# A trunk step in split fp32r on one core: the prompt's convolution as ScalarE products added in pairs by VectorE, with the weight split, w_in's tail and two norms rearranged

## The chip, the cores and the metric

The kernel runs on one core of a Trainium2 chip. The metric is device time in microseconds of one execution; the figure before is 2956.64, the median of three runs. PE is TensorE, DVE is VectorE, ACT is ScalarE, POOL is GpSimd and SP is the engine that issues the DMAs.

## The reference

One inference step of a hybrid decoder layer for 256 prompt positions and 8 x 8 sample positions, 320 columns in all, at model width 2048:

```
x1 = layer_norm(ALPHA * x + 0.5 * swiglu_ffn(x, ffn1), ln1)
proj = x1 @ w_in            # q, k, v, o, gates, glu_a, glu_b, gate_a, gate_b
h_a = mlstm_branch(q, k, v, o, ...)
u = glu_a * sigmoid(glu_b)  # depthwise convolution, 31 taps, over the positions
y = conv(concat([buf, u])) + conv_b;  h_b = silu(layer_norm(y, conv_ln))
mix = (sigmoid(gate_a) * h_a + sigmoid(gate_b) * h_b) @ w_out
x2 = layer_norm(ALPHA * x1 + mix, ln2)
y = layer_norm(ALPHA * x2 + 0.5 * swiglu_ffn(x2, ffn2), ln3)
```

The outputs are y, the new matrix memories and normalisers of the mLSTM branch, and the last 30 inputs of the convolution.

## The kernel before, in words

**Matrix products.** Activations stand as 16 tiles (k = 0 to 15) of 128 features by 320 positions. Weights come as blocks of 128 x 128, in the order in which they are used, in chunks of 8 blocks (one DMA of 512 KB each, `Stream.load`). Every fp32 product is made of three fp32r matmuls per block (`mm3`, L213 to L215): high part of the weights by the high and by the low part of the activations, then low part of the weights by the high part. `Stream._split` makes the parts: ACT copies the high part (whi, L148) and DVE subtracts it (wlo, L149), in halves of a chunk, 128 x 512, with five buffers for each and three halves made ahead.

**The order of the work.** There are 784 chunks: ffn1 (264), w_in (224), w_out (32), ffn2 (264). A group of output blocks has one accumulator in PSUM for each; the pool has five accumulators (acc) and three smaller tiles (sm). After every four blocks `tick` advances each lane by a step: lane 0 holds the gates, the heads and later the states, lane 1 norms and the finishing of the convolution, lanes 2 and 3 the convolutions by turns. `drain` emits steps of lanes until a condition holds. From the order in which the program is written, the scheduler of the tile framework makes each engine's queue; engines work in their queue's order and wait for one another by semaphores.

**w_in.** `w_in_schedule` writes the groups: first a and g of columns 0 and 1 (the inputs of the convolution), then for each further column a, g and some of q, k, v, o, ga of the heads; then a tail, gb for 16 columns, and last `oga(3)`, that is o and ga of head 3 in eight groups. A gb group's accumulator is emptied by ACT's tanh (`tanh_half`, L248), and its result multiplies the finished convolution, after its norm.

**The convolution** (`conv`, L602 to L627). ACT makes tap 0, then DVE 30 products with addition (L622, 128 x 256). The samples' part (`conv_sample`) is a product of 128 x 992 and a reduction, in two halves. Two convolutions run by turns. The 16 results are normed (`Norm`): DVE subtracts the mean (L1134) and multiplies (L1135), and ACT makes r = 1 / sqrt(v) by a logarithm and an exponential (`rsqrt`, L239 to L243).

**Starting on a norm that isn't finished** (`first_group`). The first group of w_in (4 accumulators) and of ffn2 (4) use "early" tiles eh and el, made from values to which the norm has not been applied, with two extra columns; mean and r are put in afterwards on the result (`normed`: w, late; L287 to L290). Meanwhile the normed tiles are made: L1134, L1135, xh on ACT (L500), xl on DVE (L501). In ffn2 `states` starts behind this group: 64 small matmuls (cps, L914), each followed by a DVE step into a memory tile c (L915) which DMAs load and store.

**The last norm** (`last_norm`). Centring of four tiles is done by PE (L473, L474: the tile by the identity, minus the mean of the sum), of four by POOL and of eight by DVE (L467); DVE and POOL multiply by r (L486); ACT applies gain and offset to eleven (L493) and DVE to five (L491); a DMA stores each.

Of the kernel before, what the change touches and what calls it, by code (L numbers as in the profile page):

```python
# [14 lines left out]
P = 128  # L15
# [5 lines left out]
NB = 8  # L21
# [94 lines left out]
class Stream:  # L116


    AHEAD = 3
    RAW_AHEAD = 3  # L120

    def __init__(self, nc, pool, src, n_blocks):
        self.nc, self.pool, self.src = nc, pool, src
        self.n_chunks, self.n_parts = n_blocks // CB, n_blocks // PB
        self.raw, self.parts = {}, {}
        self.next_raw = self.next_split = 0
        self.i = 0
# [12 lines left out]
    def _split(self, p):  # L140
        nc = self.nc
        c, j = divmod(p, CB // PB)
        raw = self.raw[c][:, j * PB * P:(j + 1) * PB * P]
        if (j + 1) * PB == CB:
            del self.raw[c]
        hi = self.pool.tile([P, PB * P], F32R, tag="whi", name="whi", bufs=5)
        lo = self.pool.tile([P, PB * P], F32R, tag="wlo", name="wlo", bufs=5)
        nc.scalar.activation(hi, raw, AF.Copy)  # L148
        nc.vector.tensor_tensor(out=lo, in0=raw, in1=hi.bitcast(F32), op=ALU.subtract)  # L149
        self.parts[p] = (hi, lo)  # L150

    def advance(self, p):
        while self.next_raw < min(p // (CB // PB) + self.RAW_AHEAD + 1, self.n_chunks):
            for _ in self.load():
                pass
        while self.next_split < min(p + self.AHEAD + 1, self.n_parts):
            self._split(self.next_split)
            self.next_split += 1

    def get(self):  # L160
        p, j = divmod(self.i, PB)
        if j == 0:
            self.parts.pop(p - 1, None)
            self.advance(p)
        self.i += 1
        hi, lo = self.parts[p]
        s = slice(j * P, (j + 1) * P)
        return hi[:, s], lo[:, s]


class Kernel:
    TICK = 4

    def __init__(self, tc, a):
        self.tc, self.nc, self.a = tc, tc.nc, a
        self.lanes = [collections.deque() for _ in range(4)]
# [40 lines left out]
    def gemm(self, accs, xs):  # L217

        n = len(xs)
        for k, (xh, xl) in enumerate(xs):  # L220
# [73 lines left out]
    def first_group(self, count, norm, name):  # L294

        accs = [self.acc(T + 2) for _ in range(count)]
        ys = []

        def tiles():
            for k in range(KD):  # L300
                ys.append(self.affine_split(*norm.scaled(k, name)))
                norm.z[k] = None
                yield

        self.later(tiles(), 1)
        self.gemm(accs, norm.early)
        self.drain((1,), lambda: len(ys) == KD)
        norm.early.clear()
        return [self.normed(ps, norm) for ps in accs], ys
# [9 lines left out]
    def build(self):  # L319
        tc, nc, a = self.tc, self.nc, self.a  # L320
        with (
# [11 lines left out]
            xs = []  # L333

            def x(n):
                k = len(xs)
                n = min(n, KD - k)
                raw = mp.tile([P, n * T], F32, tag="c0", name="xraw", bufs=3)
# [17 lines left out]
    def consts(self, cp):  # L356
# [3 lines left out]
        sel = self.mp.tile([ROWS, H * P], F32, tag="c0", name="selraw", bufs=3)  # L360
# [59 lines left out]
    def ffn(self, n, xs, norm=None):  # L420
# [5 lines left out]
        for kind, q, ms in ffn_schedule():  # L426
            if kind == "up":
                if xs is None:
                    accs, xs = self.first_group(2 * len(ms), norm, "ln2")
                    self.later(self.states())  # L430
# [28 lines left out]
    def last_norm(self, norm):  # L459

        nc = self.nc
        by_pe, by_pool = (0, 4, 8, 12), (3, 7, 11, 15)
        z, d = norm.z, {}

        def centre(k):
            eng = nc.gpsimd if k in by_pool else nc.vector
            eng.tensor_tensor(out=z[k], in0=z[k], in1=norm.mean, op=ALU.subtract)  # L467
            d[k] = z[k]

        with self.tc.issue_after(norm.sums.ins):  # L470
            for k in by_pe:
# [3 lines left out]
        for k in (3, 7, 1):  # L475
            centre(k)
        with self.tc.issue_after(norm.var.ins):
            for k in (2, 5, 6, 9, 11, 15):
                centre(k)
        first = None  # L480
        for k in list(d) + [k for k in range(KD) if k not in d]:
            with self.tc.issue_after((norm.last if k in d else first).ins):
                if k not in d:
                    centre(k)
                eng = nc.gpsimd if k in by_pool else nc.vector
                mul = eng.tensor_tensor(out=z[k], in0=d[k], in1=norm.r, op=ALU.mult)  # L486
                if eng is nc.vector and first is None:
                    first = mul
                g, b = self.scol("ln3_g", -0.5, k), self.col("ln3_b", k)
                if k % 3 == 1:  # L490
                    nc.vector.tensor_scalar(z[k], z[k], g, b, op0=ALU.mult, op1=ALU.add)  # L491
                else:
                    nc.scalar.activation(z[k], z[k], AF.Identity, scale=g, bias=b)  # L493
                nc.sync.dma_start(out=self.a["yT"][k], in_=z[k])
# [20 lines left out]
    def gates(self, g8):  # L515
# [60 lines left out]
        rows = mp.tile([H, R_N], F32, tag="c0", name="rows", bufs=3)  # L576
# [27 lines left out]
    def conv(self, i, acc_a, acc_g, done):  # L604
# [12 lines left out]
        nc.scalar.activation(y[:, :SEQ], pu[:, :SEQ], AF.Identity, scale=self.cw[:, i, 0:1], bias=bias)  # L617
        yield
        yield
        yp = y[:, :SEQ]  # L620
        for w in range(1, CW):
            nc.vector.scalar_tensor_tensor(out=yp, in0=pu[:, w:w + SEQ], scalar=self.cw[:, i, w:w + 1], in1=yp, op0=ALU.mult, op1=ALU.add)  # L622
            yield
            if w == 3:
                nc.sync.dma_start(out=a["conv_p"][i], in_=pu[:, SEQ:])
                nc.sync.dma_start(out=a["conv_s"][i], in_=us[:, :, NS:])
            if w in (8, 16):  # L627
                self.conv_sample(i, us, y, (w // 8 - 1) * NB // 2)
                yield
        nc.scalar.activation(y[:, SEQ:], y[:, SEQ:], AF.Identity, bias=bias)  # L630
        done(y)

    def conv_sample(self, i, us, y, b0):

        nc, n = self.nc, NB // 2
        x = self.mp.tile([P, n, NS, CW], F32, tag="taps", name="taps", bufs=1)
# [21 lines left out]
    def head(self, h, q, k, v):  # L658
# [6 lines left out]
        def load(b):  # L665
            if b < NB:
                c0[b] = mp.tile([P, 2, DV], F32, tag="c0", name="c0", bufs=3)
# [98 lines left out]
        cn = mp.tile([P, 2, DV], F32, tag="c0", name="cn", bufs=3)  # L766
# [113 lines left out]
    def states(self):  # L880
# [8 lines left out]
        def load(u):  # L889
            if u < H * NB:  # L890
                h, b = divmod(u, NB)
                c0[u] = mp.tile([P, 2, DV], F32, tag="c0", name="c0", bufs=3)
# [32 lines left out]
    def mixer(self, before):  # L925
# [33 lines left out]
        for n, group in enumerate(w_in_schedule()):  # L959
            if ys is None:  # L960
                accs, ys = self.first_group(len(group), before, "ln1")
# [3 lines left out]
            for (x, i), ps in zip(group, accs):  # L965
# [9 lines left out]
                elif x == "g":  # L975
                    self.later(self.conv(i, pend.pop(i), ps, functools.partial(conv_done, i)), 2 + i % 2)
                    self.step(self.lanes[2 + i % 2])
                elif x == "gb":
                    s = self.tanh_half(ps)
                    self.drain((2, 3, 1), lambda: self.silu_done > i)  # L980
# [239 lines left out]
```

## Time and profile before

| | us |
|---|---|
| median of 3 runs | 2956.64 (2956.19 to 2958.51) |
| the profiled execution | 2956.17 |
| its span in the trace | 2954.4 |
| PE / DVE / ACT / POOL busy | 2898.7 / 1894.8 / 1340.6 / 70.0 |
| granted PE clock, mean | 0.992 |

A row of a timeline gives start, length, engine, line, operation, output from inputs, shapes and count; a bracket behind it gives idle time before and what ended it. A row of groups gives busy time in us and the mean of one in ns. A row of waits gives the total in us, how often, and the longest. A row of stretches gives each engine's busy time with its count of instructions, then the granted clock of PE. Merged rows run back to back, so their length by their count is the pace of a queue; a single row is longer, since the end of one overlaps the start of the next.

### The profile page before, as it was taken

Reading aid. Unit: us, or ns where it says so; the run is one execution under the profiler, and the core shown is the slowest. Engines: PE = TensorE matmul, PEld = TensorE weight load, DVE = VectorE, ACT = ScalarE, POOL = GpSimd, SP = SyncE. Lnnn points to the kernel's source line nnn. Section 1 sums busy time; section 2 is a strip of 40 time slices with the busy share of each in tenths; the row PEclk is TensorE's granted clock in tenths of the full one; section 3 lists DMA queues with packets and bytes.
Section 4 is the critical chain, followed back from the end, with each engine's and each line's share of the span. In section 5 each row is a group of like instructions: output and inputs, shape, how many; then the busy total and the mean of one; then the engine's idle time right before and its main releaser. Section 6 shows DMA issues by size and latency. Waiting matters only on the chain.

```text
span 2954.4 us, 50389 instructions
## 1 busy us (share of the span) xinstructions
PE 2898.7 (98%) x19582; PEld 2868.9 (97%) x19582; DVE 1894.8 (64%) x3495; ACT 1340.6 (45%) x2384; POOL 70.0 (2%) x76
## 2 busy tenths in 40 slices
PE   9999999999999899999999989999999999999997
PEld 9999999999999899999999989998999999999997
DVE  5544444444448999989989885587454455455447
ACT  5433433433445555554554564454433433433444
POOL 0100000000000000000000000201100000000001
PEclk9999999999999999999999999999999999999999
DMA  6444444444444456554645634446455555555542
GB/s 220 150 150 150 150 150 150 150 150 151 150 150 139 125 154 194 153 170 144 202 136 174 194 116 150 150 140 223 150 183 185 198 185 196 201 181 196 176 150 103
DMA packets 171521, 483.22 MB, mean 164 GB/s; under 512 B 51308, under 2 KB 54252, under 8 KB 171280
## 3 DMA queue, kind: packets, MB, share of 16 engines
q1 hardware_dynamic: 171280, 480.00, 49.8%
q8 instruction: 153, 2.51, 0.4%
q14 instruction: 88, 0.72, 0.1%
HBM read 453.04 MB, written 26.89 MB: 162 GB/s over the span
## 4 chain that ended last, share of the span: by engine, by line
PE 96%; DVE 3%; ACT 1%; issue 0%; DMA 0%; DVEq 0%; SPq 0%; ACTq 0%
PE acc L213 31%; PE acc L214 31%; PE acc L215 31%; PE ip L822 1%; DVE z L1135 0%; PE cps L914 0%; DVE wlo L149 0%; PE num L843 0%; DVE cy L1135 0%; DVE z L486 0%; DVE xl L501 0%; PE tv L722 0%; PE sp L690 0%; PE num L214 0%; DVE cy L1134 0%
## 5 line engine op out<-in xcount | busy, mean ns | idle before, releaser
L149 DVE TENSOR_TENSOR wlo<-wraw,whi 128x512 fp32r<-128x512 f32 x1568 | 1084.6, 693 | 879.6 <-ACT whi L148 873.1
L148 ACT ACTIVATE whi<-wraw 128x512 fp32r<-128x512 f32 x1568 | 988.3, 631 | 1441.9 <-PE acc L214 1326.5
L213 PE MATMUL acc<-xh,whi 128*128 128x320 f32 x4480 | 1391.6, 311 | 25.7 <-ACT th L248 15.3
L214 PE MATMUL acc<-xl,whi 128*128 128x320 f32 x4480 | 1388.6, 310 | 6.9 <-DVE xl L501 6.9
L215 PE MATMUL acc<-xh,wlo 128*128 128x320 f32 x4480 | 1386.5, 310 | 2.7 <-DVE wlo L149 2.7
L213 PEld LDWEIGHTS acc<-xh,whi 128*128 128x128 f32 x4480 | 846.8, 189 | 31.0 <-ACT th L248 16.0
L214 PEld LDWEIGHTS acc<-xl,whi 128*128 128x128 f32 x4480 | 846.8, 189 | 13.8 <-DVE xl L501 8.6
L215 PEld LDWEIGHTS acc<-xh,wlo 128*128 128x128 f32 x4480 | 844.6, 189 | 7.1 <-DVE wlo L149 3.2
L213 PE MATMUL acc<-hh,whi 128*128 128x320 f32 x1408 | 434.4, 310 | 0.3 <-ACT whi L148 0.3
L214 PE MATMUL acc<-hl,whi 128*128 128x320 f32 x1408 | 434.0, 309 | 0.0
L215 PE MATMUL acc<-hh,wlo 128*128 128x320 f32 x1408 | 432.9, 309 | 0.0
L214 PEld LDWEIGHTS acc<-hl,whi 128*128 128x128 f32 x1408 | 264.7, 188 | 0.7
L213 PEld LDWEIGHTS acc<-hh,whi 128*128 128x128 f32 x1408 | 264.7, 188 | 0.6 <-ACT whi L148 0.6
L215 PEld LDWEIGHTS acc<-hh,wlo 128*128 128x128 f32 x1408 | 264.2, 188 | 0.0
L622 DVE SCALAR_TENSOR_TENSOR cy<-pu,cw,cy 128x256 f32<-128x256 f32 x480 | 220.9, 480 | 1.2
L448 DVE SCALAR_TENSOR_TENSOR z<-acc,z 128x320 f32<-128x320 f32 x128 | 62.7, 490 | 51.5 <-PE acc L215 49.8
L214 PE MATMUL acc<-ml,whi 128*128 128x320 f32 x256 | 79.2, 310 | 0.0
L213 PE MATMUL acc<-mh,whi 128*128 128x320 f32 x256 | 79.0, 309 | 0.0
L215 PE MATMUL acc<-mh,wlo 128*128 128x320 f32 x256 | 78.7, 309 | 0.0
L438 DVE TENSOR_TENSOR h<-s,acc 128x320 f32<-128x320 f32 x86 | 42.0, 488 | 51.9 <-ACT s L436 51.9
L315 POOL TENSOR_TENSOR z<-xh,xl 128x320 f32<-128x320 f32 x48 | 60.0, 1256 | 621.3 <-DVE h L438 357.1
L436 ACT ACTIVATE s<-acc 128x320 f32<-128x320 f32 x86 | 37.6, 438 | 69.0 <-PE acc L215 69.0
(290 smaller groups left out, 1655.1 us busy)
## 6 DMA issues: line engine op xcount, KB each, us to landing
wraw<-in_wst SPq DMA_DIRECT2D x783, 512.0 KB, 3.3
c<-in_C SPq DMA_DIRECT2D x64, 512.0 KB, 4.4
out_C_s<-c SPq DMA_DIRECT2D x32, 512.0 KB, 3.3
out_yT<-z SPq DMA_DIRECT2D x16, 160.0 KB, 1.9
out_C_p<-cn SPq DMA_DIRECT2D x4, 512.0 KB, 3.0
kv<-vst SPq DMA_DIRECT2D x8, 256.0 KB, 4.9
vst<-kv SPq DMA_DIRECT2D x8, 256.0 KB, 3.2
us<-in_cache SPq DMA_DIRECT2D x16, 120.0 KB, 3.1
```

Of the source, the lines that this page charges most:

```text
L148: nc.scalar.activation(hi, raw, AF.Copy)
L149: nc.vector.tensor_tensor(out=lo, in0=raw, in1=hi.bitcast(F32), op=ALU.subtract)
L213: mm(ps, hi, xh, start=first, stop=False)
L214: mm(ps, hi, xl, start=False, stop=False)
L215: mm(ps, lo, xh, start=False, stop=last)
L315: self.nc.gpsimd.tensor_tensor(out=t, in0=hi.bitcast(F32), in1=lo.bitcast(F32), op=ALU.add)
L436: nc.scalar.activation(s, accs[2 * j], AF.Silu)
L438: nc.vector.tensor_tensor(out=hh, in0=s, in1=accs[2 * j + 1], op=ALU.mult)
L448: nc.vector.scalar_tensor_tensor(out=z[m], in0=ps, scalar=0.5 / ALPHA, in1=z[m], op0=ALU.mult, op1=ALU.add)
L622: nc.vector.scalar_tensor_tensor(out=yp, in0=pu[:, w:w + SEQ], scalar=self.cw[:, i, w:w + 1], in1=yp, op0=ALU.mult, op1=ALU.add)
L822: mm(ip[:32, :], qc[j][:, bs], x, start=j == 0 and n == 0, stop=j == 1 and n == 1)
```

## The change

Four things change together.

1. `conv`: ACT makes 30 products in pairs, side by side in tiles of 128 x 2 x 256; DVE adds the pairs (14 adds of 128 x 512), makes the last tap and adds the two halves. The samples' part comes in four parts of 128 x 496. One lane holds all convolutions one after another, and before the third and every later one starts, the last but one is drained.
2. `Stream`: whole chunks are split at once (128 x 1024; the first two chunks still in halves), with three buffers for each part, two chunks ahead.
3. `w_in_schedule`: in each step the other groups come ahead of a and g, and the tail is `oga(3)`, then the 16 gb groups.
4. `first_groups`: in ffn2 the first two up groups (4 accumulators, then one accumulator and one small PSUM tile) use the early tiles, and `states` starts behind the second. `last_norm`: PE centres nine tiles, DVE seven, POOL none; DVE multiplies in the order of k, and ACT applies gain and offset to all 16.

The ring c0 of large tiles goes from three buffers to two, with some of its users on another tag.

```
-        groups += [[("a", i)], [("g", i)]]
         upto = len(others) * (n + 1) // len(steps)
         groups += [[x] for x in others[done:upto]]
         done = upto
-    tail = [("gb", j) for j in range(KD)] + oga(3)
+        groups += [[("a", i)], [("g", i)]]
+    tail = oga(3) + [("gb", j) for j in range(KD)]
...
+        hi = self.pool.tile([P, CB * P], F32R, tag="whi", name="whi", bufs=3)
+        lo = self.pool.tile([P, CB * P], F32R, tag="wlo", name="wlo", bufs=3)
+        n = PB * P if c < 2 else CB * P
+        for i in range(0, CB * P, n):
+            s = slice(i, i + n)
+            nc.scalar.activation(hi[:, s], raw[:, s], AF.Copy)
+            nc.vector.tensor_tensor(out=lo[:, s], in0=raw[:, s], in1=hi[:, s].bitcast(F32), op=ALU.subtract)
...
+        accs = [self.acc(T + 2) for _ in range(4)]
         self.later(tiles(), 1)
-        self.gemm(accs, norm.early)
+        self.gemm(accs, norm.early, not more)
+        if more:
+            yield [self.normed(ps, norm) for ps in accs]
+            del accs
+            accs = [self.acc(T + 2)] + [self.sm([P, T + 2], "acc") for _ in range(more - 1)]
+            self.gemm(accs, norm.early, True)
...
-        for w in range(1, CW):
-            nc.vector.scalar_tensor_tensor(out=yp, in0=pu[:, w:w + SEQ], scalar=self.cw[:, i, w:w + 1], in1=yp, op0=ALU.mult, op1=ALU.add)
+        two = mp.tile([P, 2, SEQ], F32, tag="sums", name="sums", bufs=2)
+        for w in range(0, CW - 1, 2):
+            x = mp.tile([P, 2, SEQ], F32, tag="taps", name="tap", bufs=3) if w else two
+            for j in range(2):
+                f, more = (AF.Copy, {}) if w + j else (AF.Identity, {"bias": bias})
+                nc.scalar.activation(x[:, j, :], pu[:, w + j:w + j + SEQ], f, scale=self.cw[:, i, w + j:w + j + 1], **more)
+            if w:
+                nc.vector.tensor_tensor(out=two, in0=two, in1=x, op=ALU.add)
             yield
...
-        by_pe, by_pool = (0, 4, 8, 12), (3, 7, 11, 15)
+        by_pe = (0, 1, 2, 4, 6, 8, 10, 12, 14)
+        by_dve = [k for k in range(KD) if k not in by_pe]
...
-                    self.later(self.conv(i, pend.pop(i), ps, functools.partial(conv_done, i)), 2 + i % 2)
-                    self.step(self.lanes[2 + i % 2])
+                    self.drain((2,), lambda: i < 2 or cy[i - 2] is not None)
+                    conv = self.conv(i, pend.pop(i), ps, functools.partial(conv_done, i))
+                    next(conv)
+                    self.later(conv, 2)
```

The order on the engines, at three places. First DVE at the start of ffn2, where the normed tiles (xl), the weights' low parts (wlo), the states' steps (c) and the afterwards-normed results (late) share its queue. Before, from the twelfth xl on:

```order
L915 SCALAR_TENSOR_TENSOR c_22712<-c_22712,wc,cps 128x512
L501 SCALAR_TENSOR_TENSOR xl<-z,par,xh 128x320
L915 SCALAR_TENSOR_TENSOR c_23039<-c_23039,wc,cps 128x512 x2
L501 SCALAR_TENSOR_TENSOR xl<-z,par,xh 128x320 x3
L289 TENSOR_TENSOR late<-acc,r 128x320 x4
L915 SCALAR_TENSOR_TENSOR c_23278<-c_23278,wc,cps 128x512 x2
```

And now, at the same part of its work:

```order
L512 SCALAR_TENSOR_TENSOR xl<-z,par,xh 128x320
L153 TENSOR_TENSOR wlo<-wraw,whi 128x1024
L512 SCALAR_TENSOR_TENSOR xl<-z,par,xh 128x320 x2
L936 SCALAR_TENSOR_TENSOR c_21300<-c_21300,wc,cps 128x512 x2
L153 TENSOR_TENSOR wlo<-wraw,whi 128x1024
L512 SCALAR_TENSOR_TENSOR xl<-z,par,xh 128x320
L296 TENSOR_TENSOR late<-acc,r 128x320 x4
L153 TENSOR_TENSOR wlo<-wraw,whi 128x1024
```

Fewer of the states' steps stand there, and a whole chunk's wlo stands between the other steps; the three wlo are those of chunks 530, 531 and 532.

Second ACT in w_in's tail, behind the conv norm's r. The names th<-cy and th<-acc are the tanh of a normed conv tile and of a gate's accumulator. Before:

```order
L148 ACTIVATE whi<-wraw 128x512 x4
L248 ACTIVATE th<-cy,conv_ln_b_scaled 128x320
L253 ACTIVATE th<-th 128x320
L148 ACTIVATE whi<-wraw 128x512
L263 ACTIVATE mh<-hv 128x320
L248 ACTIVATE th<-cy,conv_ln_b_scaled 128x320 x4
L248 ACTIVATE th<-acc 128x320
```

And now:

```order
L152 ACTIVATE whi<-wraw 128x1024 x3
L255 ACTIVATE th<-cy,conv_ln_b_scaled 128x320 x2
L260 ACTIVATE th<-th 128x320
L255 ACTIVATE th<-cy,conv_ln_b_scaled 128x320
L255 ACTIVATE th<-acc 128x320
```

The accumulator's tanh now stands behind three conv pieces where it stood behind six steps that wait for one another; the accumulator is that of ga's column 14, where it was one of the gb groups.

Third PE at the end, where z is a tile of the last norm, ps and pq its mean and mean square, cst the identity. Before:

```order
L1119 MATMUL ps<-ns,mean_d 128x320
L1120 MATMUL pq<-sq,mean_d 128x320
L473 MATMUL acc<-z,cst 128x320
L474 MATMUL acc<-ns,minus_mean 128x320
L473 MATMUL acc<-z,cst 128x320
```

And now, directly behind the last matmul of ffn2:

```order
L498 MATMUL acc<-z,cst 128x320 x5
L1142 MATMUL ps<-ns,mean_d 128x320
L499 MATMUL acc<-ns,minus_mean 128x320 x5
L1143 MATMUL pq<-sq,mean_d 128x320
L498 MATMUL acc<-z,cst 128x320
```

Five centring matmuls moved ahead of the mean and five between it and the mean square.

More of the change, by code (lines that the diff above doesn't have):

```diff
@@ L138, in load, with _split, advance @@
         self.raw[c] = t
-    def _split(self, p):
+    def _split(self, c):
         nc = self.nc
[L142 to L153, printed above, removed]
+        raw = self.raw.pop(c)
+        hi = self.pool.tile([P, CB * P], F32R, tag="whi", name="whi", bufs=3)
[5 more added lines that the diff above has]
+            nc.vector.tensor_tensor(out=lo[:, s], in0=raw[:, s], in1=hi[:, s].bitcast(F32), op=ALU.subtract)
+        self.parts[c] = (hi, lo)
+    def advance(self, c):
+        while self.next_raw < min(c + self.RAW_AHEAD + 1, self.n_chunks):
             for _ in self.load():
                 pass
-        while self.next_split < min(p + self.AHEAD + 1, self.n_parts):
+        while self.next_split < min(c + self.AHEAD + 1, self.n_chunks):
             self._split(self.next_split)
@@ L292, in normed, with first_groups @@
         return t
-    def first_group(self, count, norm, name):
-        accs = [self.acc(T + 2) for _ in range(count)]
+    def first_groups(self, norm, name, more=0):
         ys = []
@@ L425, in ffn @@
         new = Norm(self, z, EPS / ALPHA ** 2, "ln1" if n == 1 else None, KD)
-        for kind, q, ms in ffn_schedule():
+        first = None if xs else self.first_groups(norm, "ln2", 2)
+        for i, (kind, q, ms) in enumerate(ffn_schedule()):
             if kind == "up":
-                if xs is None:
-                    accs, xs = self.first_group(2 * len(ms), norm, "ln2")
-                    self.later(self.states())
+                if first and i < 2:
+                    accs = next(first)
+                    if i == 1:
+                        xs = next(first)
+                        self.later(self.states())
                 else:
@@ L461, in last_norm @@
         nc = self.nc
-        by_pe, by_pool = (0, 4, 8, 12), (3, 7, 11, 15)
+        by_pe = (0, 1, 2, 4, 6, 8, 10, 12, 14)
+        by_dve = [k for k in range(KD) if k not in by_pe]
         z, d = norm.z, {}
         def centre(k):
-            eng = nc.gpsimd if k in by_pool else nc.vector
-            eng.tensor_tensor(out=z[k], in0=z[k], in1=norm.mean, op=ALU.subtract)
             d[k] = z[k]
-        with self.tc.issue_after(norm.sums.ins):
-            for k in by_pe:
+            return nc.vector.tensor_tensor(out=z[k], in0=z[k], in1=norm.mean, op=ALU.subtract)
+        with self.tc.issue_after(norm.var.ins):
+            for k in by_dve[:3]:
+                centre(k)
+        prev = norm.last
+        for k in range(KD):
+            if k in by_pe:
                 d[k] = self.acc()
@@ L474, in last_norm @@
                 nc.tensor.matmul(d[k], self.minus_mean, norm.s, start=False, stop=True)
[L475 to L482, printed above, removed]
+            with self.tc.issue_after(prev.ins):
                 if k not in d:
                     centre(k)
[L485 to L494, printed above, removed]
+                prev = nc.vector.tensor_tensor(out=z[k], in0=d[k], in1=norm.r, op=ALU.mult)
+            nc.scalar.activation(z[k], z[k], AF.Identity, scale=self.scol("ln3_g", -0.5, k), bias=self.col("ln3_b", k))
+            nc.sync.dma_start(out=self.a["yT"][k], in_=z[k])
     def affine_split(self, u, b):
@@ L575, in gates @@
             yield
-        rows = mp.tile([H, R_N], F32, tag="c0", name="rows", bufs=3)
+        rows = mp.tile([H, R_N], F32, tag="c0", name="rows", bufs=2)
         mrow, wk, em, wr = (rows[:, o:o + n] for o, n in ((R_M, T), (R_K, T), (R_E, T), (R_W, TS)))
@@ L666, in load @@
             if b < NB:
-                c0[b] = mp.tile([P, 2, DV], F32, tag="c0", name="c0", bufs=3)
+                c0[b] = mp.tile([P, 2, DV], F32, tag="c0", name="c0", bufs=2)
                 nc.sync.dma_start(out=c0[b], in_=a["C0"][b, h])
@@ L764, in head @@
         yield
-        cn = mp.tile([P, 2, DV], F32, tag="c0", name="cn", bufs=3)
+        cn = mp.tile([P, 2, DV], F32, tag="c0", name="cn", bufs=2)
         for j in range(2):
```

61 lines of the change are left out of this document (36 added, 25 removed).

## The prediction

> **What bounds the kernel now.** I read the page's busy line first, then stretches of 60 us, then who waits for whom, and last the order of time at the three places where TensorE falls behind.
>
> ```profile
> span 2954.4 us, 50389 instructions
> PE 2898.7 (98%) x19582; PEld 2868.9 (97%) x19582; DVE 1894.8 (64%) x3495; ACT 1340.6 (45%) x2384; POOL 70.0 (2%) x76
> ```
>
> TensorE is the bound almost everywhere. DVE's 64% and ACT's 45% are averages, so the stretches matter (columns: PE, PEld, DVE, ACT, POOL busy with counts, granted clock, DMA share, GB/s).
>
> ```profile
> 660.00:720.00 60.00, 60.00 (x410) 60.00 (x409) 28.43 (x46) 22.30 (x36) 0.00 (x0) 1.00 0.44 150
> 960.00:1020.00 60.00, 51.44 (x339) 48.12 (x338) 56.93 (x116) 32.34 (x63) 0.00 (x0) 0.91 0.42 122
> 1320.00:1380.00 60.00, 57.24 (x378) 56.29 (x377) 50.62 (x107) 33.10 (x66) 0.00 (x0) 0.97 0.49 140
> 1620.00:1680.00 60.00, 60.00 (x407) 56.97 (x407) 55.06 (x107) 34.08 (x63) 0.00 (x0) 1.00 0.66 203
> 1680.00:1740.00 60.00, 47.80 (x309) 47.28 (x308) 49.22 (x102) 34.11 (x64) 0.00 (x0) 0.89 0.34 114
> 1980.00:2040.00 60.00, 55.60 (x339) 52.18 (x338) 56.88 (x123) 33.01 (x63) 2.13 (x2) 0.94 0.59 197
> ```
>
> An undisturbed stretch holds about 409 matmuls, 0.147 us each, so a chunk (8 blocks, 24 matmuls) takes 3.53 us. In the mixer's steady part DVE is busy for 55 of 60 us and TensorE still loses nothing: relieving DVE there is worth nothing by itself. What is to be had is in the stretches that fall short. At 0.147 us for each missing matmul: 960 (start of w_in) 10.3, 1320 (a head's norm) 4.6, 1680 (w_in's gb groups) 14.7, 1980 (start of ffn2) 10.3, of which about 1 is eleven cps matmuls that are 512 wide (by width 0.235 each), so 9.3.
>
> ```profile
> PE acc L213 <- ACT th L248: 15.3, 3, 10.8
> PE acc L214 <- DVE xl L501: 6.9, 5, 5.7
> PE tv L722 <- ACT v L968: 1.3, 1, 1.3
> PE pb L674 <- DVE parts L599: 1.1, 1, 1.1
> PE acc L213 <- ACT k L968: 0.9, 1, 0.9
> ```
>
> The waits name the same places. The 10.8 us one is in the gb groups, the 5.7 at w_in's start. The rest of the first row (15.3 - 10.8 = 4.5) with the last three is 7.8 us of small waits around gates and heads.
>
> **The convolution.** ACT had one of a conv's 31 taps and gets 30. DVE gives up 29 of its 30 products for 14 adds of double width and a fold. A conv has 21 steps and 24 ticks pass in its period, so the drain before the next but one rarely has anything left to emit.
>
> ```profile
> L149 DVE TENSOR_TENSOR wlo<-wraw,whi 128x512 fp32r<-128x512 f32 x1568 | 1084.6, 693 | 879.6 <-ACT whi L148 873.1
> L148 ACT ACTIVATE whi<-wraw 128x512 fp32r<-128x512 f32 x1568 | 988.3, 631 | 1441.9 <-PE acc L214 1326.5
> L622 DVE SCALAR_TENSOR_TENSOR cy<-pu,cw,cy 128x256 f32<-128x256 f32 x480 | 220.9, 480 | 1.2
> 997.88 0.88 DVE L622 SCALAR_TENSOR_TENSOR cy<-pu,cw,cy 128x256 f32<-128x256 f32 x2
> 1722.71 0.55 ACT L248 ACTIVATE th<-cy,conv_ln_b_scaled 128x320 f32<-128x320 f32 x1
> 1732.55 1.90 ACT L248 ACTIVATE th<-cy,conv_ln_b_scaled 128x320 f32<-128x320 f32 x4
> 1718.61 1.14 ACT L148 ACTIVATE whi<-wraw 128x512 fp32r<-128x512 f32 x2
> 1992.63 1.90 DVE L149 TENSOR_TENSOR wlo<-wraw,whi 128x512 fp32r<-128x512 f32 x3
> ```
>
> Back to back an L622 takes 0.40 us (two in 0.88, alone 0.48 in the mean), so 29 of them are 11.6 us. The adds of 128x512 resemble wlo, 0.60 each (three in 1.90, alone 0.69): 14 x 0.60 + 0.35 for the fold = 8.8. The sample's taps in four parts cost two more starts. DVE saves under 3 us per conv, all of it beside TensorE's work: nothing. ACT needs a budget. A conv period is 6 groups of 16 blocks, 12 chunks, 42.4 us. Whole-chunk whi takes at most the 1.14 us of two halves: 13.7. Other ACT work is 34.08 less 34 halves at 0.631, 12.6 in 60 us, so 8.9. A product takes about 0.45 (four 320-wide ones in 1.90, alone 0.55): 13.5. Together 36.1 of 42.4, 85%. It fits; ACT may then finish 15% before it is needed. Its in-order queue has whi behind products, but whi for three whole chunks is kept, as far ahead (7 us) as five halves were. Cost taken: 0. If that cover goes, see the third rival. Splitting in whole chunks saves a fixed part per pair of halves on both engines, off the path too.
>
> The Trainium skill, page ScalarE: Activation LUTs, section Rules for kernel authors, speaks against this: multiplications belong on VectorE, up to about three times faster. That is stated for bf16 single-source work. The trace's rows, 0.40 for the DVE product and 0.45 for a wider ACT one, show no such gap here; by the page's section What ACT_TABLE_LOAD costs a 256-wide product is an estimated 0.40 us, and the sum above would not change.
>
> **The w_in tail: -13.5 us.** Now gb comes straight behind the last conv, and gb's accumulators cannot be emptied while ACT's tanh for them waits behind the conv norm.
>
> ```profile
> 1722.05 7.49 DVE L1135 SCALAR_TENSOR_TENSOR cy<-cy,conv_ln_g_scaled,r 128x320 f32<-128x320 f32 x16
> 1734.35 0.41 ACT L248 ACTIVATE th<-acc 128x320 f32<-128x320 f32 x1
> 1734.82 0.64 PE L213 MATMUL acc<-xh,whi 128*128 128x320 f32 x1 [10.78 <-ACT th L248]
> ```
>
> TensorE stands 10.78 us and then runs at half clock (0.89 over the stretch). With oga(3) ahead, eight groups of 16 blocks, 56 us, need nothing of the conv, and the norm (statistics, two table loads, the 7.49 us row) runs under them. The order puts ga14's tanh behind three tanh pieces and the whi of chunk 461, which starts when TensorE has left chunk 458: 3.5 us later 1.14 for whi, then four pieces at 0.45, while its accumulator is wanted another chunk on. I get 7.0 us after the end of chunk 457 against 7.06 wanted. DVE, whose 16-piece run stands between wlo 460 and 461, gets wlo 461 done 11.4 us after that point, against 10.6 + 0.6 wanted. So 0 to 1.5 us stays; I take 1.2 of 14.7.
>
> **The start of ffn2: -7.3 us.** The early (unnormalised) tiles now feed 96 blocks, not 64, and the states begin behind them.
>
> ```profile
> 1984.59 3.71 DVE L1134 TENSOR_TENSOR z<-z,mean 128x320 f32<-128x320 f32 x9
> 1998.41 5.65 DVE L1135 SCALAR_TENSOR_TENSOR z<-z,ln_g_scaled,r 128x320 f32<-128x320 f32 x12
> 2016.36 1.42 DVE L915 SCALAR_TENSOR_TENSOR c<-c,wc,cps 128x512 f32<-128x512 f32 x2
> 2023.83 0.70 DVE L149 TENSOR_TENSOR wlo<-wraw,whi 128x512 fp32r<-128x512 f32 x1
> 2010.00:2015.00 5.00, 2.94 (x14) 2.02 (x14) 5.00 (x15) 1.00 (x2) 0.00 (x0) 1.00 0.40 130
> 2015.00:2020.00 5.00, 3.02 (x8) 1.60 (x9) 5.00 (x11) 0.00 (x0) 0.00 (x0) 0.67 0.39 136
> ```
>
> ```profile
> PE acc L215 <- DVE wlo L149: 1.3, 1, 1.3
> ```
>
> DVE is the late one: from 1984 it never rests, and 9 steps of L915 (about 0.7 each) and the late tiles stand ahead of the wlo that TensorE wants. In the changed order only 2 of these steps stand ahead of chunk 531's wlo. I followed DVE from the statistics on: centre 0.41, L1135 0.47, xl the same, L915 0.7, whole wlo 1.2 (two at 0.60). The tightest place: wlo 527 can end 2.3 us after TensorE leaves chunk 524 (1.1 for whi, 1.2), then 15 L1135 (7.0), mr 0.4 and wlo 528 (1.2) make 10.9, wanted at 3 x 3.53 + 0.6 = 11.2. Chunks 529 to 531 have 0.3 to 1 us to spare, later ones more. So the wait nearly goes, with nothing in hand: I take 2 us left of 9.3, bounds 0 and 9.
>
> In the two 5 us rows TensorE issues 14 and 8 matmuls and the clock falls to 0.67, though the longest wait that the list for 1980 to 2040 has is 1.3 us (its first row, above; the others are shorter). The Trainium skill, page TensorE: Matmul & The Clock Gate, section Part 1: The HAM clock gate, has half rate follow an idle window of about 3.4 us; read as full idleness that would rule out a throttle for the short waits that I leave. The trace says that a half-filled window is enough, so a few 1 us waits in a row could cost another 1.7 us (a third of 5), within the bounds.
>
> **The last norm: +0.8 us.** POOL loses its eight steps and DVE's centring gets faster, but the order puts TensorE's own centring first.
>
> ```profile
> 2933.01 0.81 PE L1119 MATMUL ps<-ns,mean_d 128*128 128x320 f32 x2 [1.11 <-DVE ns L1043]
> 2933.66 0.70 PE L1120 MATMUL pq<-sq,mean_d 128*128 128x320 f32 x2
> 2934.20 0.70 PE L473 MATMUL acc<-z,cst 128*128 128x320 f32 x2
> 2934.47 0.49 DVE L1124 SCALAR_TENSOR_TENSOR v<-pq,v 128x320 f32<-128x320 f32 x1 [1.01 <-PE pq L1120]
> 2934.88 4.71 DVE L467 TENSOR_TENSOR z<-z,mean 128x320 f32<-128x320 f32 x5
> 2936.05 0.47 ACT L241 ACTIVATE rsq<-r 128x320 f32<-128x320 f32 x1
> 2940.61 1.29 DVE L486 TENSOR_TENSOR z<-acc,r 128x320 f32<-128x320 f32 x3
> 2944.84 3.38 ACT L493 ACTIVATE z<-z,par,ln_g_scaled 128x320 f32<-128x320 f32 x6 [0.41 <-DVE z L486]
> 2949.53 0.65 ACT L493 ACTIVATE z<-z,par,ln_g_scaled 128x320 f32<-128x320 f32 x1 [1.30 <-DVE z L486]
> ```
>
> Each of these fp32 matmuls takes 0.54 us. TensorE is free at 2931.75; five of them end at 2934.4, then ps, then five more, so pq starts at 2937.6, not 2933.66. v follows 0.81 later, at 2938.4; it takes 0.49 and ACT's three steps end 1.56 behind it (2936.52 now, from 2934.96), 2940.5, and three centrings at 0.41 hide under them. Two DVE steps at about 0.5 give the first product at 2941.6 against 2940.61. Then 16 affine pieces on ACT at 0.55 (six in 3.38, alone 0.65) from 2942.2 end at 2951.0, where now the last ends at 2950.18: +0.8, bounds -1 and +2.
>
> **Others.** w_in's start keeps its DVE order (15 scalings, then xl): 0, bounds -1 and +1. Emptying accumulators gets further ahead at heads and gates, but two table loads per head stay and ACT is fuller: of the 7.8 us I take 4, bounds -8 and +5. Start of the kernel, tags, the c0 ring of two: 0; a c tile's way out and back ends before its next use by this order.
>
> Sum: -13.5 - 7.3 + 0.8 - 4 = -24.0. The profiled execution took 2956.17 (1.8 outside its span), so 2932.2; the median of the runs is 0.5 higher, so about 2932.5.
>
> **The rivals.** First, ffn2's start is not gained: DVE has 0.3 us in hand there over 35 us of unbroken work, and 3% longer steps give the waits and the half clock back. 2932.5 + 7.3, about 2940. Against it: 32 more early blocks are 14 us of cover. Chance 0.17.
>
> Second, the gb groups still wait for the norm, for half the price: the same 16-piece run on DVE, and slack under 1 us on ACT. 2932.5 + 7, about 2940. Against it: 56 us of cover. Chance 0.1.
>
> Third, slower: ACT becomes the mixer's bound. Its period fills at (42.4 - 13.7 - 8.9) / 30 = 0.66 us per product; beyond, each 0.01 costs 0.3 us per conv, 14 periods, 4.2 us. It eats the 24 us at 0.72, and at 0.75 the time is 2932.5 + 38, about 2970. For it: a lone ACT piece with scale and bias takes 0.65 in the last row above, and each pair waits for DVE's add. Against: 0.45 back to back. The skill's ScalarE rule, named above, points this way. Chance 0.06.
>
> A change without effect is out as a mechanism (the orders differ), but losses could cancel gains: 0.05.
>
> **How the numbers follow.** Forecast 0.62. The measurement tells 0.2%, 5.9 us. Forecast and the first two rivals are all faster than 2950.7, even together at 2947. The sum's favourable bounds give about 2922, both rivals together 2947. So 2922 to 2947; faster 0.86, same 0.07, slower 0.07.
>
> **What would show it.** Right: 1680 to 1740 holds about 400 matmuls at clock 1.00 and the 10.8 us wait is gone; ffn2's first 60 us miss under 25; the first last-norm product comes later behind pq than now; ACT near 50 of 60 us in the mixer with no wait for whi. Wrong: PE waits for whi or wlo spread over the mixer (third rival), clock under 1 at ffn2's start (first), or PE waiting for a tanh in the gb groups (second).

## The result, and the profile after

| | before | changed |
|---|---|---|
| median, us | 2956.41 (2956.09 to 2958.51, 4 runs) | 2928.81 (2928.00 to 2929.26, 4 runs) |
| the profiled execution | 2956.17 | 2929.01 |
| its span | 2954.4 | 2927.2 |

The ratio is 0.9904, 95% interval 0.9892 to 0.9916: faster by 27.6 us. The forecast was 2932.5 within 2922 to 2947.

The same stretches as before, of the changed kernel (PE, PEld, DVE, ACT, POOL busy with counts, granted clock, DMA share, GB/s):

```profile
660.00:720.00 60.00, 60.00 (x412) 60.00 (x411) 26.17 (x29) 18.72 (x19) 0.00 (x0) 1.00 0.46 153
960.00:1020.00 60.00, 51.84 (x332) 48.95 (x331) 54.33 (x99) 45.09 (x89) 0.13 (x1) 0.91 0.43 112
1020.00:1080.00 60.00, 60.00 (x410) 58.59 (x410) 56.63 (x123) 46.52 (x90) 0.12 (x1) 1.00 0.51 155
1320.00:1380.00 60.00, 60.00 (x409) 59.30 (x409) 57.13 (x105) 45.93 (x92) 0.12 (x1) 1.00 0.51 154
1680.00:1740.00 60.00, 60.00 (x409) 59.81 (x408) 49.37 (x83) 43.03 (x72) 0.00 (x0) 1.00 0.44 136
1740.00:1800.00 60.00, 58.28 (x397) 58.02 (x396) 48.49 (x80) 36.84 (x68) 0.00 (x0) 1.00 0.48 157
1980.00:2040.00 60.00, 60.00 (x404) 59.56 (x403) 51.97 (x88) 31.90 (x49) 6.93 (x6) 1.00 0.71 242
```

Of the four stretches that the prediction priced one is still short: w_in's start has 332 matmuls and a clock of 0.91. The gb groups run at full clock with 409 where 309 stood, and 1740 to 1800, where the conv norm now falls, lacks only 12 of 409. ffn2's start has 404, of which ten are the 512-wide cps. One stretch is new: 1260 to 1320, which had 407 before, has 400. The waits of PE, whole kernel:

```profile
PE acc L218 <- DVE xl L512: 6.4, 2, 5.9
PE acc L217 <- ACT whi L152: 6.2, 2, 4.9
PE acc L498 <- DVE z L503: 3.8, 1, 3.8
PE acc L217 <- ACT xh L511: 1.8, 1, 1.8
PE acc L217 <- ACT th L255: 1.7, 1, 1.7
PE acc L219 <- DVE wlo L153: 1.7, 1, 1.7
```

The first and the fourth are w_in's start, the second the first matmuls of the kernel, the third the last norm, where PE waits for accumulators and nobody for PE. The tanh row, 15.3 us before, is 1.7: one wait at a head, at 1307. The last row is the conv norm.

### The profile page after: what moved, and what is told of

Read it like the earlier page. It is cut to its first block, busy times and chain, and to the rows that moved or that the text cites. A ratio compares the mean times of both kernels' runs of the same rounds, so it can differ in the third digit from the quotient of the medians.

```text
span 2927.2 us, 47986 instructions
## 1 busy us (share of the span) xinstructions
PE 2899.9 (99%) x19602; PEld 2871.0 (98%) x19602; DVE 1750.6 (60%) x2557; ACT 1360.2 (46%) x2073; POOL 49.3 (2%) x68
## 4 chain that ended last, share of the span: by engine, by line
PE 98%; DVE 1%; DMA 1%; ACT 0%; issue 0%; SPq 0%; ACTq 0%; DVEq 0%
PE acc L219 31%; PE acc L217 31%; PE acc L218 31%; PE ip L843 1%; PE cps L935 1%; DMA xraw<-in_xT 0%; ACT z L504 0%; DVE z L1158 0%; PE sp L711 0%; PE num L864 0%; DMA wraw<-in_wst 0%; PE num L219 0%; PE num L218 0%; DVE cy L1158 0%; PE tv L743 0%; DVE wlo L153 0%
## 5 line engine op out<-in xcount | busy, mean ns | idle before, releaser
L153 DVE TENSOR_TENSOR wlo<-wraw,whi 128x1024 fp32r<-128x1024 f32 (+1 forms) x786 | 967.1, 1231 | 846.5 <-ACT whi L152 845.4
L152 ACT ACTIVATE whi<-wraw 128x1024 fp32r<-128x1024 f32 (+1 forms) x786 | 830.2, 1056 | 1268.5 <-PE acc L218 1002.3
L217 PE MATMUL acc<-xh,whi 128*128 128x320 f32 x4448 | 1376.2, 310 | 9.7 <-ACT whi L152 6.2
L218 PE MATMUL acc<-xl,whi 128*128 128x320 f32 x4448 | 1374.8, 309 | 6.4 <-DVE xl L512 6.4
L217 PEld LDWEIGHTS acc<-xh,whi 128*128 128x128 f32 x4448 | 838.3, 189 | 14.5 <-ACT whi L152 6.5
L218 PEld LDWEIGHTS acc<-xl,whi 128*128 128x128 f32 x4448 | 837.1, 188 | 12.2 <-DVE xl L512 7.2
L219 PEld LDWEIGHTS acc<-xh,wlo 128*128 128x128 f32 x4448 | 835.7, 188 | 5.7 <-DVE wlo L153 2.2
L635 ACT ACTIVATE tap<-pu,cw 128x256 f32<-128x256 f32 x448 | 194.6, 498 | 10.4 <-DVE sums L637 9.9
L637 DVE TENSOR_TENSOR sums<-sums,tap 128x512 f32<-128x512 f32 x224 | 153.8, 687 | 8.8 <-ACT tap L635 4.4
```

Of the source, the lines that this page charges most:

```text
L152: nc.scalar.activation(hi[:, s], raw[:, s], AF.Copy)
L153: nc.vector.tensor_tensor(out=lo[:, s], in0=raw[:, s], in1=hi[:, s].bitcast(F32), op=ALU.subtract)
L217: mm(ps, hi, xh, start=first, stop=False)
L218: mm(ps, hi, xl, start=False, stop=False)
L219: mm(ps, lo, xh, start=False, stop=last)
L635: nc.scalar.activation(x[:, j, :], pu[:, w + j:w + j + SEQ], f, scale=self.cw[:, i, w + j:w + j + 1], **more)
```

## The experiments

Each time stands beside the median of the kernel before on the same chip (2956.9 to 2957.2); four single edits of the kernel before come first, then edits of the changed one. The changed kernel itself ran on another occasion (2928.81 against 2956.41), so a difference of a few us from it is compared through the ratios to the kernel before. The interval of a ratio reaches about 4 us to each side; where two of them overlap, the text says what else supports the difference.

**The tail alone.**

```
-    tail = [("gb", j) for j in range(KD)] + oga(3)
+    tail = oga(3) + [("gb", j) for j in range(KD)]
```

Expected: 

> The kernel before with one edit: w_in's tail is oga(3), then the gb groups. Theory (each place has its own stall, and the tail's is cured by eight groups that need nothing of the convolution): the 10.8 us wait for the gate's tanh is gone, the stretch that held 309 matmuls holds over 395, and the time falls by 13 us, 11 to 15, to about 2943. Rival (the convolution's load on DVE is what makes the norm late, and taking it off brings the gain): the wait only moves to another group and the fall is under 5 us.

Measured: 2944.35 against 2957.20, ratio 0.9957 (0.9942 to 0.9972), 12.9 us less. Its stretch in the gb groups:

```profile
1680.00:1740.00 60.00, 60.00 (x411) 59.91 (x410) 52.45 (x109) 41.85 (x82) 0.00 (x0) 1.00 0.43 140
```

411 matmuls where 309 stood, with the convolution still on DVE. The theory holds, the rival falls: no lighter DVE was needed. At 0.147 us the 102 matmuls are 15.0 us; part of the 2.1 us that the time doesn't show is lost at the start of ffn2, where 1980 to 2040 now has 336 matmuls at a clock of 0.91 (339 at 0.94 before).

**Two early groups in ffn2 alone.**

```
+                if more and k % 3 == 2:
+                    yield
...
+            accs = [self.acc(T + 2)] + [self.sm([P, T + 2], "acc") for _ in range(more - 1)]
+            self.gemm(accs, norm.early, True)
...
```

Expected: 

> The kernel before with one edit: ffn2's first two up groups use the early tiles and the states begin behind them. Theory: the start of ffn2 gains 9 us, 7 to 10, nothing else moves, about 2947. Rival (it needs the split in whole chunks or a lighter DVE too): under 4 us, with PE still waiting for xl or wlo there.

Measured: 2948.04 against 2957.20, ratio 0.9970 (0.9960 to 0.9981), 9.2 us less. The start of ffn2:

```profile
1980.00:2040.00 60.00, 60.00 (x404) 59.69 (x403) 57.98 (x129) 37.63 (x72) 0.88 (x1) 1.00 0.55 183
```

DVE is as full as before, 57.98 of 60, and PE loses nothing: the edit is enough, with the old split. It brings 32 more early blocks, and with them the states start later and the normed tiles are made at a slower pace (the first two lines); these three were not tried apart.

**The last norm alone** (the new `last_norm`, nothing else).

Expected: 

> The kernel before with one edit: the new last norm (nine tiles centred by PE, none by POOL, all affine pieces on ACT). Theory: the first product comes about 1 us later behind ffn2's last matmul, as five centring matmuls stand ahead of the mean and five behind it, and a tighter end gives that back: between -1 and +1 us, no difference that can be told. Rival (what POOL held up on DVE was the end's bound): 2 to 4 us less.

Measured: 2957.33 against 2957.20, ratio 1.0001 (0.9992 to 1.0010). No difference; POOL was not the bound of the end.

**The convolution alone** (the new `conv` and `conv_sample`, one lane, the drain).

Expected: 

> The kernel before with one edit: the convolution as ACT products in pairs, one at a time. Theory: DVE falls from 55 to about 50 of 60 us in the mixer and ACT rises from 34 to about 48, and as PE waited for neither there, the time stays within 4 us of before; the 10.8 us wait in the gb groups stays. Rival (DVE's load was behind the small waits and the tail): 8 us less or more than that.

Measured: 2955.76 against 2957.20, ratio 0.9995 (0.9986 to 1.0005). The time is the theory's, but not because nothing happened. Its stretches:

```profile
960.00:1020.00 60.00, 44.91 (x276) 42.37 (x276) 55.83 (x111) 44.85 (x98) 0.12 (x1) 0.88 0.37 109
1320.00:1380.00 60.00, 59.19 (x402) 58.47 (x401) 51.11 (x107) 47.01 (x101) 0.12 (x1) 1.00 0.47 146
1620.00:1680.00 60.00, 60.00 (x406) 57.20 (x405) 47.09 (x83) 45.14 (x95) 0.00 (x0) 1.00 0.68 209
1680.00:1740.00 60.00, 47.10 (x304) 46.58 (x303) 46.53 (x97) 31.44 (x58) 0.00 (x0) 0.88 0.34 110
```

In the stretch at 1620 DVE falls from 55.06 to 47.09 and ACT rises from 34.08 to 45.14, and PE does 406 matmuls where it did 407. One stretch overstates the fall of DVE: over the 540 us from 1100 to 1640 DVE goes from 489.4 to 460.3 and ACT from 293.3 to 415.2, which is 54.4 to 51.1 and 32.6 to 46.1 of each 60 us, near the expected 50 and 48. The stretch at 1320 gains 24 matmuls (3.5 us), those at 1020 and 1380 gain 21 and 13, and the one at 960 loses 63 (9.3 us): gains at the gates and heads, and a new stand near 1010, which the old order of the steps, below, has too.

**The convolution back on DVE, in the changed kernel** (the old `conv`, `conv_sample` and two lanes).

Expected: 

> The changed kernel with the convolution back on DVE (scalar products with addition, two at a time), the rest as changed. The four edits tried singly leave about 4 us of the whole gain unaccounted for. Theory: the convolution is worth nothing here either, 0 to +3 us over the changed kernel (2929 to 2932), since PE waits for neither engine in the mixer. Rival (the edits help one another, a lighter DVE gives the head and gate waits back): +4 to +10, with waits of 2 to 5 us for a tanh, and DVE near 55 of 60 us.

Measured: 2926.71 against 2957.04, ratio 0.9899 (0.9884 to 0.9913); runs from 2926.05 to 2926.90. Not slower, and by its runs 2.1 us faster than the changed kernel, although the two ratios' intervals overlap; a second pair below, with PE's centring held back in both, gives 2.0 (2924.44 and 2922.48). By these two pairs theory and rival both had the sign wrong. In its trace PE waits for no tanh of 1 us or more, and the stand at 1307 of the changed kernel is gone. ACT's queue there, in the changed kernel:

```profile
1303.36 1.06 ACT L152 ACTIVATE whi<-wraw 128x1024 fp32r<-128x1024 f32 x1 [2.10 <-issue]
1304.44 1.28 ACT L246 ACT_TABLE_LOAD   x1
1306.35 0.47 ACT L246 ACTIVATE rsq<-v 128x320 f32<-128x320 f32 x1 [0.62 <-DVE v L897]
1306.84 1.28 ACT L247 ACT_TABLE_LOAD   x1
1308.13 0.47 ACT L247 ACTIVATE rs<-rsq 128x320 f32<-128x320 f32 x1
1308.51 0.42 ACT L255 ACTIVATE th<-acc 128x320 f32<-128x320 f32 x1
```

The accumulator's tanh stands behind a head's two table loads and its norm, and PE stands from 1306.94 to 1308.98. There are no products in these rows. So it isn't a product that holds this tanh up; that the convolution's place changes the order around it is the reading that is left, and it was not tested by itself.

**The old order of the steps, in the changed kernel.**

```
-        groups += [[x] for x in others[done:upto]]
-        done = upto
         groups += [[("a", i)], [("g", i)]]
+        groups += [[x] for x in others[done:upto]]
+        done = upto
```

Expected: 

> The changed kernel with a and g ahead of the heads' groups again in each of w_in's steps (one edit). Theory: the rest of the gain that no single edit gave comes from the heads' groups standing earlier, so that accumulators behind a head's norm have more cover; putting it back costs 3 to 5 us, as waits for a tanh near the heads. Rival (it comes from the convolution's move or the whole-chunk split): 0, within 1.5 us.

Measured: 2948.39 against 2957.04, ratio 0.9971 (0.9961 to 0.9982). It costs 19.6 us, four times what was expected. Two stands make it. The first, PE from 1010.52 to 1017.71, on ACT:

```profile
1008.13 2.50 ACT L635 ACTIVATE tap<-pu,cw 128x256 f32<-128x256 f32 x6
1010.72 1.06 ACT L152 ACTIVATE whi<-wraw 128x1024 fp32r<-128x1024 f32 x1
1011.68 0.89 ACT L635 ACTIVATE tap<-pu,cw 128x256 f32<-128x256 f32 x2
1013.72 0.91 ACT L635 ACTIVATE tap<-pu,cw 128x256 f32<-128x256 f32 x2 [1.16 <-DVE sums L637]
...
1016.43 0.91 ACT L635 ACTIVATE tap<-pu,cw 128x256 f32<-128x256 f32 x2 [0.68 <-DVE sums L637]
1017.24 0.41 ACT L255 ACTIVATE th<-acc 128x320 f32<-128x320 f32 x1
```

With a2 and g2 right behind the first group, the drain ahead of the third convolution emits what is left of the first one in a row, and the accumulators' tanh comes behind it: product waits for sum, sum for product. The convolution alone, above, has the same stand: PE waits 6.3 us for a tanh there. The second stand, 10.3 us at 1725, is two norms that meet:

```profile
1713.52 0.47 ACT L247 ACTIVATE rs<-rsq 128x320 f32<-128x320 f32 x1
...
1723.44 1.28 ACT L246 ACT_TABLE_LOAD   x1
...
1729.55 0.47 ACT L247 ACTIVATE r<-rsq 128x320 f32<-128x320 f32 x1
...
1735.50 0.41 ACT L255 ACTIVATE th<-acc 128x320 f32<-128x320 f32 x1
```

rs is head 3's norm and r the convolution's, 16 us apart; in the changed kernel it is 45 (1690.43 and 1735.17). Between rs and the convolution's norm one tanh of an accumulator stands (at 1713.89); the next is the one at 1735.50, behind that norm, and PE waits 9.99 us for it.

**The old steps and the old convolution together, in the changed kernel.**

Expected: 

> The changed kernel with the old step order (a and g ahead of the heads' groups) and also the old convolution on DVE, two at a time. The old step order alone cost 19.6 us: a stand of 7.2 at 1010, where ACT works off products that the drain before the third convolution emits in a row, and one of 10.3 at 1725, where head 3's norm and the convolution's norm lie 16 us apart on ACT instead of 45. Theory: both come from convolutions drained one at a time; with two lanes and no drain both go, about 2929, within 4 us of the changed kernel. Rival (the step order by itself brings the two norms together): the stand at 1725 stays, 2938 or more.

Measured: 2929.89 against 2956.94, ratio 0.9908 (0.9893 to 0.9922). Both stands are gone, and the theory's number is met. Its reason is met only for the first: the two norms lie 20 us apart here as well (1699.44 and 1719.71) with no long wait, so their distance alone doesn't make the stand at 1725. What differs is where the tanh of the accumulators stand: four of them come between the two norms here (from 1699.82 to 1705.15), one in the kernel with the stand. Why the scheduler puts them so was not settled. Against the kernel with the old convolution and the new steps (2926.71) the old steps cost 3.2 us: its list has two waits of 1.3 us between 1020 and 1080, where the kernel before had three, and the other kernel has none.

**PE's centring held behind the sums, in the changed kernel.**

```
-                nc.tensor.matmul(d[k], self.ident, z[k], start=True, stop=False)
-                nc.tensor.matmul(d[k], self.minus_mean, norm.s, start=False, stop=True)
+                with self.tc.issue_after(norm.sums.ins):
+                    nc.tensor.matmul(d[k], self.ident, z[k], start=True, stop=False)
+                    nc.tensor.matmul(d[k], self.minus_mean, norm.s, start=False, stop=True)
```

Expected: 

> The changed kernel, with PE's centring matmuls of the last norm held behind the mean and the mean square. Theory (the ten centring matmuls delay the variance by about 4 us, and DVE and ACT then need the same time as before): the first product comes 6.2 us behind ffn2's last matmul instead of 10.0, and the time falls by 3.8 us, 3 to 4.5, to 2925. Rival (the end is bound by ACT's 16 pieces and the stores, and PE's tiles then come too late): under 1.5 us.

Measured: 2924.44 against 2957.04, ratio 0.9891 (0.9876 to 0.9906), 4.4 us less than the changed kernel by the medians; the intervals overlap, and the two traces show where it comes from. The end of the changed kernel, and of this one:

```profile
2904.67 0.31 PE L219 MATMUL acc<-hh,wlo 128*128 128x320 f32 x1
2904.82 2.85 PE L498 MATMUL acc<-z,cst 128*128 128x320 f32 x10
2907.51 0.70 PE L1142 MATMUL ps<-ns,mean_d 128*128 128x320 f32 x2
2908.05 2.86 PE L499 MATMUL acc<-ns,minus_mean 128*128 128x320 f32 x10
2910.74 0.70 PE L1143 MATMUL pq<-sq,mean_d 128*128 128x320 f32 x2
2914.69 1.29 DVE L503 TENSOR_TENSOR z<-acc,r 128x320 f32<-128x320 f32 x3
2915.22 8.83 ACT L504 ACTIVATE z<-z,par,ln_g_scaled 128x320 f32<-128x320 f32 x16 [1.61 <-DVE z L503]
```

```profile
2903.25 0.31 PE L219 MATMUL acc<-hh,wlo 128*128 128x320 f32 x1
2904.67 0.81 PE L1143 MATMUL ps<-ns,mean_d 128*128 128x320 f32 x2 [1.11 <-DVE ns L1067]
2905.31 0.70 PE L1144 MATMUL pq<-sq,mean_d 128*128 128x320 f32 x2
2909.33 1.29 DVE L504 TENSOR_TENSOR z<-acc,r 128x320 f32<-128x320 f32 x3
2909.86 8.83 ACT L505 ACTIVATE z<-z,par,ln_g_scaled 128x320 f32<-128x320 f32 x16 [1.68 <-DVE z L504]
```

pq stands 6.07 us behind ffn2's last matmul in the first and 2.06 in the second, and the first product follows at 10.02 and 6.08, so 3.9 us are this place. ACT's 16 pieces take 8.83 in both, and the rival falls.

**Two early groups in w_in too, in the changed kernel.**

```
-    groups = [[("a", 0), ("g", 0), ("a", 1), ("g", 1)]]
+    groups = [[("a", 0), ("g", 0), ("a", 1), ("g", 1)], others[:2]]
...
```

Expected: 

> The changed kernel with ffn2's cure applied to w_in's start: the first q group has two accumulators and is the second one on early tiles (32 more blocks, 14 us). Theory: the 11.4 us that PE loses at 960 to 980 (waits of 5.9, 1.8 and half clock) fall to under 3, so the time falls by 9, 7 to 11, to 2920. Rival (xl and xh come still later because more tiles are held, or the gates and the first convolutions are pushed into new waits): under 4 us.

Measured: 2927.03 against 2957.04, ratio 0.9903 (0.9886 to 0.9919); runs from 2925.87 to 2929.35: 1.8 us less by the medians, which these runs can't tell from none, and not 9. The 960 stretch goes from 332 to 365 matmuls:

```profile
960.00:1020.00 60.00, 55.97 (x365) 53.37 (x364) 54.99 (x98) 45.25 (x89) 0.00 (x0) 0.97 0.43 129
```

And in its list of PE's waits a new row (sum, count, longest):

```profile
PE acc L217 <- DVE late L296: 2.9, 1, 2.9
```

The wait for xl is gone, and the next one is for the accumulators: the groups on early tiles hold them until DVE has made `late`, which it does behind twelve of the sixteen xl. PE stands 3.2 us there (980.17 to 983.40). Further, the waits for a tanh at 1260 to 1330 are 3.6 us where the changed kernel has 1.7. The rival's bound holds, and of its two reasons the new waits.

**The halves again, in the changed kernel** (the old `Stream`).

Expected: 

> The changed kernel with the split in halves of a chunk again, five buffers of each part. Theory: the fixed parts saved lie off the path, except at ffn2's start, where DVE has 0.3 us in hand by the working and 1.5 to 2 more are needed for the halves: 0 to +3 us, 2929 to 2932. Rival (the whole chunk is what keeps ACT and DVE under their limit in the mixer): +5 or more, with waits for whi or wlo over the mixer.

Measured: 2923.48 against 2956.94, ratio 0.9886 (0.9872 to 0.9901); runs from 2922.64 to 2924.89: 5.3 us faster than the changed kernel by the medians, again with the sign against theory and rival. The intervals just overlap; the runs of the changed kernel lie from 2928.00 to 2929.26. The two waits of the changed kernel at 1307 and 1749 are gone (2.0 us each at PE). At 1749, the changed kernel's DVE:

```profile
1739.55 2.36 DVE L153 TENSOR_TENSOR wlo<-wraw,whi 128x1024 fp32r<-128x1024 f32 x2
1742.35 7.50 DVE L1158 SCALAR_TENSOR_TENSOR cy<-cy,conv_ln_g_scaled,r 128x320 f32<-128x320 f32 x16
1749.75 1.23 DVE L153 TENSOR_TENSOR wlo<-wraw,whi 128x1024 fp32r<-128x1024 f32 x1
```

PE waits until 1751.04 for a part whose first half would have been there 0.5 us earlier. With halves the run of 16 is also broken: a half's wlo stands behind its fourteenth and one behind its fifteenth step (1736.74 and 1737.80). How the 2.0 us divide between the two was not tried, and the other 1.3 us of the 5.3 were not traced to a place.

**The faster edits together.** First the old convolution and PE's centring behind the sums:

Expected: 

> The changed kernel with two edits that each were faster singly: the convolution back on DVE (-2.1) and PE's last centring behind the sums (-4.4). Theory: they sit at different places and add: 2922.3, 2921 to 2924. Rival: they share something, and the time is that of the better one, 2924.4.

Measured: 2922.48 against 2956.94, ratio 0.9882 (0.9868 to 0.9897): by the medians they add. Then w_in's two early groups as well:

Expected: 

> The kernel of the two edits with a third, the second group of w_in on early tiles, which alone gave 1.8 us instead of the 9 expected: its stand at 960 was gone, but 6 us of new ones came at 980 to 1000 and 2.4 at 1280, some of them waits for a tanh on ACT. Theory: with the products off ACT the waits for a tanh go and the edit gives 4 to 6 us, 2916 to 2919. Rival (the new waits are for accumulators that the second group holds): again about 2 us, 2920 to 2921.

Measured: 2920.94 against 2956.94, ratio 0.9878 (0.9861 to 0.9894): 1.5 us less again, the rival's number. This is the fastest of the kernels tried, 7.9 us under the changed one. The halves were not tried together with these.

## Why the prediction was right, point by point

The bound was read rightly: in the mixer's steady part PE waited for neither DVE nor ACT, and the gain came from the places where it stood, the two large ones shown by an edit each. In the whole change the split and the order of the steps were not tried alone in the kernel before. The terms, in us; the measured ones are the matmuls missing by stretch at 0.147, and the single edit's change:

| term | forecast | in the changed kernel | edit alone |
|---|---|---|---|
| w_in's tail | -13.5 | -12.9 (309 to 409, less 12 behind 1740) | -12.9 |
| start of ffn2 | -7.3 | -9.3 (no wait left) | -9.2 |
| heads and gates | -4 | -7 | - |
| last norm | +0.8 | -0.3 | +0.1 |
| convolution | 0 | +2.1 (undoing it gains 2.1) | -1.4 |
| whole-chunk split | 0 | +5.3 (undoing it gains 5.3) | - |
| start of w_in | 0 | +1.0 (339 to 332) | - |

**The tail.** The residue was worked out from DVE's run of 16 between two wlo; the trace has just that run and a wait of 1.7 for a wlo behind it, 0.2 over the 0 to 1.5 that was given. With halves, in the edit alone, 1740 to 1800 has 412 matmuls and no such wait. The tanh of ga14 cost nothing.

**ffn2's start.** The chain of sums with 0.3 us in hand came out on the safe side: no wait of PE is in the list there, and the rival of 3% longer steps didn't come. The 2 us left over were caution. Nothing there depended on the split, since the edit alone gave the same. As no short waits were left, what a row of them would have done to the clock wasn't put to the test.

**The last norm.** The delay of the first product was forecast as 1.0 and is 1.0 (9.02 to 10.02 behind the last matmul of ffn2). The missing 1.1 is behind it: before, the span ended 4.2 us after ACT's last piece, now 3.15 (2924.05 to 2927.2). The last store is issued 1.28 us behind that piece before and 0.35 now: before, ACT and DVE finished pieces side by side and their stores queued, now they leave one by one. The prediction names as a sign that the first product comes later behind pq than before. That didn't happen and doesn't follow from its sums: the product stood 6.95 us behind pq and stands 3.95 behind it now, against 4.0 in the working. What comes later is pq itself.

**Heads and gates.** Half of them was taken, as a guess with no chain of steps behind it, and they are mostly gone, 7.8 us of waits before and 1.7 now. That the total came so near owes something to luck: before, the stretch at 1020 was short too,

```profile
1020.00:1080.00 60.00, 56.26 (x380) 55.16 (x379) 59.22 (x147) 30.59 (x58) 0.25 (x2) 1.00 0.49 146
```

and now has 410, 4.4 us, as 1320 has 31 more, 4.6; so 9.0 were gained where 4 was taken, and 2.0 of them came back at 1307 with the convolution and the split, which were taken at nothing. Two misses partly cancel. The part at 1020 to 1060 is the order of the steps by the pair that differs in it alone (2929.89 and 2926.71, 383 and 410 matmuls). For 1320 no single edit is needed: the convolution alone brings it from 378 to 402, and the kernel with the old convolution and the old steps but whole chunks has 404, while the tail, ffn2's start and the last norm alone leave it at 378 or 379. Whether that is the split or the ring c0, the other difference that none of these edits covers, was not tried.

**The convolution and the split** were costed at nothing, and that is the step that missed: off the path in the steady part, but not at the norms, where one ACT queue serves tanh, table loads and whi, and one DVE queue the norm's run and wlo. DVE's saving was sized well, under 3 us per conv, and is 2.2 by the convolution alone (1894.8 to 1860.2 us busy, over 16). ACT's load was overrated: 44.2 of each 60 us from 1100 to 1640 instead of 51. Most of that is the period of a conv, taken as twelve chunks, 42.4 us. The starts of the second and the sixteenth conv lie 700.4 us apart, 50.0 for each of 14 periods, since the weights' matmuls there, some 4080 at 0.147, make 600 of them and the heads' own matmuls nearly all the rest. So the third rival's limit was (50.0 - 13.7 - 10.5) / 30 = 0.86 us per product, not 0.66. A smaller part is that a product takes 0.40 back to back, not 0.45:

```profile
L635 ACT ACTIVATE tap<-pu,cw 128x256 f32<-128x256 f32 x448 | 194.6, 498 | 10.4 <-DVE sums L637 9.9 <-DVE cy L664 0.2
1001.18 2.49 ACT L635 ACTIVATE tap<-pu,cw 128x256 f32<-128x256 f32 x6
```

(Six in 2.49, alone 0.50.) That is the 0.40 which the Trainium skill, page ScalarE: Activation LUTs, section What ACT_TABLE_LOAD costs, gives by its formula; the trace agrees. The rule of the Trainium skill, same page, section Rules for kernel authors, to leave multiplications on VectorE is not borne out by pace here, as both engines take 0.40. In the changed kernel the convolution with its products on ScalarE costs 2.1 us, in the kernel before it saves 1.4, which is within the noise.

The terms of the third column that are measured by stretch make -28.5, the spans differ by 27.2; the remaining 1.3 was not traced to places. The effects of undoing lie inside these and don't add to them.

## What to carry to other kernels

Where one engine is busy 98% of the time, price an edit only at the places where that engine stands, and there follow the one queue that it waits for step by step; the two large terms came out within 2 us that way, and the term that was guessed missed by 3. Independent work put ahead of a chain of norms was worth nearly the whole stall in w_in's tail and at ffn2's start, and needed no lighter engine; at w_in's start it gave at most 2 of 9 us, where the groups put ahead held the accumulators that the next ones needed, a new wait of 2.9 us. Moving or merging work on an engine that waits elsewhere isn't free just because the engine has time on average: in-order queues make the larger piece, or a run emitted by a drain, stand before the small one that frees an accumulator.

## What the runs showed of the hardware that was not expected

Doubling a DVE step's width saves little: two halves of wlo back to back take 1.20 us, a whole one 1.13 (two in 2.36, alone 1.23), so 0.07 us per chunk were won, and a step that could have stood between the halves comes up to 0.6 us later (an estimate, one half's 0.60). An fp32 matmul of 320 columns costs PE 0.54 us (ten merged rows, five instructions, in 2.85), as the prediction took it, against 0.147 for an fp32r one, so ten of them for centring were as long as 37 of the product's, and holding them back was worth 4.4 us.
